# Hybrid attention / SSD / convolution block: the decays inside the SSD's chunks computed by scans on VectorE over rows spread by DMA, in place of split products with triangles on TensorE

## The chip, the cores and the metric

The kernel runs on one core of one Trainium2 chip. The time is the device time of one execution in microseconds (us); the page and the trace below come from one further execution that was profiled. TensorE (PE, with its weight loads as PEld), VectorE (DVE), ScalarE (ACT), GpSimd (POOL) and SyncE (SP, which here issues all the DMAs) run side by side, each through its own queue in its own fixed order.

## The reference

Two layers, each on 512 latent and 256 context tokens of 1024 channels. A layer projects the normalised input, feeds three branches (attention, a bidirectional SSD, a convolution module), gates and merges them, and projects back. The part that matters here is the SSD's work inside a chunk of 128 tokens, for 8 heads and two directions:

```
def segsum(x):
    t = x.shape[-1]
    xe = jnp.broadcast_to(x[..., :, None], x.shape + (t,))
    xs = jnp.cumsum(jnp.where(jnp.tril(jnp.ones((t, t), bool), -1), xe, 0.0), axis=-2)
    return jnp.where(jnp.tril(jnp.ones((t, t), bool)), xs, -jnp.inf)
...
    a = (dt * a_head).reshape(b, nc, SSD_CHUNK, h).transpose(0, 3, 1, 2)
...
    lmat = jnp.exp(segsum(a)).astype(x.dtype)
    cb = jnp.einsum('bclhn,bcshn->bhcls', cc, bc)
    y_diag = jnp.einsum('bhcls,bcshp->bclhp', cb * lmat, xd)
```

So for each chunk, head and direction a 128 x 128 matrix is needed whose entry (s, l) is the sum of `a` over the tokens after s up to l. Its exponential is the decay from token s to token l.

## The kernel before

All matrix products of the projections are made in three TensorE passes over split numbers: each weight tile is loaded as float32 (`raw`, three buffers), ScalarE rounds it (`whi`, L156), VectorE takes the rest (`wlo`, L157), and the matmuls run hh x whi, hh x wlo, hl x whi (`mm_cm_steps`, L175). The order on TensorE is written out by hand for most of a layer (`manual_schedule`). The other engines' orders and the DMA queue's are set by the scheduler of the framework from its own estimate of the times, with priorities; weight loads have a high one.

The SSD's inner loop stands in `Chunk` and in the list `main`. The first layer has 6 chunks (two of context, four latent), the second has 4. Each chunk has `begin` (L741, the products of C and B, masked into `gm`), two `decay(g)` (L751, one for each group of 4 heads), two `inner(g)` (L777, the matmuls `pyd` that use the weights `wt` of `decay`) and `end` (L790). That is 12 decays in the first layer and 8 in the second, 20 in all. `inner(g)` comes two steps behind its `decay(g)` (`ahead = 2`), and after every step `sf.fill` gives TensorE a piece of other work: the merge of the convolution branch (`merge_steps`, tiles `ps_gm` and `ps_br`) and the attention gates (`ps_ga`). So TensorE always has projections between the SSD's steps.

One `decay(g)` does this for each of the two directions: ScalarE makes four tiles `am` (a triangle of ones times the rounded `da` of a head, L759), VectorE makes `al` (the same triangle times the rest of `da`, L761), and TensorE multiplies `am` and `al` by a strict triangle (L764). All four products add up in one PSUM bank, `pseg`, which then holds for each head the forward sums above the diagonal and the backward sums below it. ScalarE takes the exponential (`ew`, L767), VectorE and ScalarE build `wt` from `gm` and the step sizes (L771, L772) and multiply by `ew` (L774):

```
for j, part in enumerate((am, al)):
    T.matmul(pseg[:, 0:512], m_gt if d == 0 else m_lt, part.rearrange("p h l -> p (h l)"),
             start=(d == 0 and j == 0), stop=(d == 1 and j == 1))
```

`small` (L83) gives tiles of 2 KB a partition from a ring of seven called W2. `am`, `al`, `ew`, `wt`, `xd` (the states' input, L722), the pieces of q and k on their way (`qs`, `qhl`, `khl`), `pth` of attention, the residual rows `xr` and others share it. `y0` (L781) is the one large GpSimd operation of a chunk.

Of the kernel before, what the change touches and what calls it, by code (L numbers as in the profile page):

```python
# [9 lines left out]
F32 = mybir.dt.float32  # L10
# [5 lines left out]
P = 128  # L16
# [41 lines left out]
def hybrid_kernel(ctx, tc, xT, cc, consts, rope, mod_params, params, fnw, w_mod, w_cm, w_q, w_kvd, w_z,  # L58
# [24 lines left out]
    def small(shape, dt, name):  # L83
        return wk.tile(shape, dt, tag="W2", name=name, bufs=7)
# [40 lines left out]
    mr = const.tile([P, 3 * P], F32R, name="mr")  # L125
    S.activation(mr, mraw, AF.Copy)
    m_gt, m_lt, identr = mr[:, 0:P], mr[:, P:2 * P], mr[:, 2 * P:3 * P]
# [185 lines left out]
    z_dr = [dr.tile([P, 512], F32, name=f"zdr{k}") for k in range(NTT)]  # L313
    y_dr = [dr.tile([P, NT], F32, name=f"ydr{k}") for k in range(KD)]

    mods = [sm.tile([P, 24, 2], F32, tag="mod", name=f"mod{i}", bufs=2) for i in range(2)]
    for li in range(2):
# [127 lines left out]
        na = sm.tile([P, 16], F32, tag="na", name="na")  # L445
        S.activation(na, par[:, O_AL:O_AL + 16], AF.Exp)
# [33 lines left out]
        dah = sm.tile([P, NTT, 16], F32R, tag="dah", name="dah")  # L480
        dal = sm.tile([P, NTT, 16], F32, tag="dal", name="dal")
        V.tensor_copy(dah, da)
        V.tensor_tensor(out=dal, in0=da, in1=f(dah), op=ALU.subtract)

# [67 lines left out]

        pc = pot("pc_cum")
# [3 lines left out]
        T.matmul(pcv[:, 1, :, 0:8], f(m_gt), da[:, :, 0:8], start=True, stop=True)  # L557
        T.matmul(pcv[:, 1, :, 8:16], f(m_lt), da[:, :, 8:16], start=True, stop=True)
# [176 lines left out]
        class Chunk:  # L735
# [15 lines left out]
            def decay(self, g):  # L751

                c, gm2 = self.c, self.gm2
                pseg = pwt("pseg")
                for d, m in enumerate((m_le, m_ge)):
                    h0 = d * 8 + g * 4
                    am = small([P, 4, P], F32R, "am")
                    for i in range(4):
                        S.activation(am[:, i, :], m, AF.Copy, scale=f(dah)[:, c, h0 + i:h0 + i + 1])  # L759
                    al = small([P, 4, P], F32R, "al")  # L760
                    V.tensor_tensor(out=al, in0=m.unsqueeze(1).to_broadcast([P, 4, P]),  # L761
                                    in1=dal[:, c, h0:h0 + 4].unsqueeze(2).to_broadcast([P, 4, P]), op=ALU.mult)
                    for j, part in enumerate((am, al)):
                        T.matmul(pseg[:, 0:512], m_gt if d == 0 else m_lt, part.rearrange("p h l -> p (h l)"),  # L764
                                 start=(d == 0 and j == 0), stop=(d == 1 and j == 1))
# [496 lines left out]
```

## Time and profile before

| | |
|---|---|
| median of 3 runs | 1495.2 us (1494.25 to 1498.19) |
| the profiled execution's own time | 1495.54 us |
| its span | 1493.8 us |
| busy: PE, PEld, DVE, ACT, POOL | 1450.1, 1255.5, 1039.1, 721.9, 81.6 us |
| PE busy by fortieths of the span | 5999999999999999999999989999999999999997 |
| moved by DMA | 172.58 MB, 116 GB/s over the span |

The span is what the profiler saw between the first and the last instruction; 1.7 us of the execution's time lie around it. Busy time counts an instruction from its start to its end. Matmuls overlap each other, so TensorE's pace is read from the distance between the starts of two matmuls, not from the length of one. An engine's idle time is listed with what ended it.

### The profile page before, as it was taken

How to read it: one execution, taken by the hardware profiler on the slowest of the kernel's cores; microseconds unless marked ns; L12 is line 12 of the kernel's file. 1: busy time of each engine (PE TensorE's matmuls, PEld its weight loads, DVE VectorE, ACT ScalarE, POOL GpSimd, SP SyncE). 2: the span in 40 equal slices, each digit the busy share in tenths (PEclk: the TensorE clock that was granted, in tenths of full speed). 3: DMA queues.
4: the chain of work that ended last, by engine and by line, in shares of the span. 5: the costliest groups of instructions: out<-in, count | busy, mean ns of one | idle time of the engine just before them, and what ended most of it. 6: DMA issues, size and time to landing. Idle time of an engine off the chain costs nothing.

```text
span 1493.8 us, 25061 instructions
## 1 busy us (share of the span) xinstructions
PE 1450.1 (97%) x9716; PEld 1255.5 (84%) x9716; DVE 1039.1 (70%) x1911; ACT 721.9 (48%) x1624; POOL 81.6 (5%) x177
## 2 busy tenths in 40 slices
PE   5999999999999999999999989999999999999997
PEld 4889899988888888888888877989988887888886
DVE  4689998666568675555344377899977788666564
ACT  4423543364445475555333154355455557666341
POOL 0000010100002110000000000001010021000000
PEclk9999999999999999999999999999999999999998
DMA  9222333223233322323652532213423242322542
GB/s 377 69 72 94 108 117 111 76 71 103 100 114 123 124 94 99 121 64 121 226 176 92 173 114 86 82 57 110 152 78 106 96 151 78 105 85 91 185 141 78
DMA packets 69687, 172.58 MB, mean 116 GB/s; under 512 B 7872, under 2 KB 24384, under 8 KB 69568
## 3 DMA queue, kind: packets, MB, share of 16 engines
q1 hardware_dynamic: 69568, 170.98, 34.8%
q8 instruction: 76, 1.25, 0.3%
q14 instruction: 43, 0.35, 0.1%
HBM read 143.43 MB, written 27.53 MB: 114 GB/s over the span
## 4 chain that ended last, share of the span: by engine, by line
PE 91%; DMA 2%; DVE 2%; ACT 2%; issue 1%; SPq 0%; POOL 0%; POOLq 0%; DVEq 0%; ACTq 0%
PE ps_gm L175 23%; PE ps_br L175 11%; PE ps_xbc L175 9%; PE ps_o L175 6%; PE ps_gcv L175 4%; PE ps_g L175 4%; PE ps_u L175 4%; PE po_v L1042 3%; PE ps_ga L175 3%; PE pt_p L1028 3%; PE ps_l L982 2%; PE ps_mod L229 2%; PE ps_z L216 1%; PE ps_q L216 1%; PE ps_q L217 1%; PE ps_z L217 1%
## 5 line engine op out<-in xcount | busy, mean ns | idle before, releaser
L156 ACT ACTIVATE whi<-raw 128x512 fp32r<-128x512 f32 (+1 forms) x316 | 199.0, 632 | 280.8 <-PE ps_gm L175 63.8
L157 DVE TENSOR_TENSOR wlo<-raw,whi 128x512 fp32r<-128x512 f32 (+1 forms) x316 | 216.9, 690 | 148.0 <-ACT whi L156 144.0
L175 PE MATMUL ps_gm<-hh,whi 128*128 128x512 f32 (+1 forms) x576 | 212.6, 369 | 0.0
L408 DVE SCALAR_TENSOR_TENSOR vacc<-vt,par,vacc 128x783 f32<-128x783 f32 (+1 forms) x232 | 206.5, 890 | 8.1 <-ACT vacc L405 4.5
L175 PE MATMUL ps_gm<-hh,wlo 128*128 128x512 f32 (+1 forms) x576 | 210.1, 365 | 0.0
L175 PE MATMUL ps_gm<-hl,whi 128*128 128x512 f32 (+1 forms) x576 | 209.6, 364 | 0.0
L175 PEld LDWEIGHTS ps_gm<-hh,whi 128*128 128x128 f32 x576 | 109.0, 189 | 16.4 <-issue 3.1
L175 PEld LDWEIGHTS ps_gm<-hh,wlo 128*128 128x128 f32 x576 | 109.0, 189 | 15.1 <-issue 1.7
L175 PEld LDWEIGHTS ps_gm<-hl,whi 128*128 128x128 f32 x576 | 109.0, 189 | 13.8 <-issue 0.9
L175 PE MATMUL ps_xbc<-hh,whi 128*128 128x512 f32 (+1 forms) x240 | 83.0, 346 | 0.0
L175 PE MATMUL ps_xbc<-hh,wlo 128*128 128x512 f32 (+1 forms) x240 | 82.1, 342 | 0.0
L175 PE MATMUL ps_xbc<-hl,whi 128*128 128x512 f32 (+1 forms) x240 | 82.0, 342 | 0.0
L1034 ACT ACTIVATE pth<-pt_p 128x512 f32<-128x512 f32 x72 | 43.6, 605 | 55.8 <-PE pt_p L1028 55.7
L653 ACT ACTIVATE tg<-ps_gm,hw 128x512 f32<-128x512 f32 x72 | 44.2, 614 | 51.1 <-PE ps_gm L175 51.1
L175 PE MATMUL ps_o<-yh,whi 128*128 128x256 f32 (+1 forms) x208 | 65.8, 317 | 1.5 <-DVE xnew L1105 1.4
L175 PE MATMUL ps_o<-yl,whi 128*128 128x256 f32 (+1 forms) x208 | 65.7, 316 | 0.0
L175 PE MATMUL ps_o<-yh,wlo 128*128 128x256 f32 (+1 forms) x208 | 65.7, 316 | 0.0
L522 DVE SCALAR_TENSOR_TENSOR xacc<-xraw,par,xacc 128x770 f32<-128x770 f32 (+1 forms) x64 | 63.4, 999 | 3.0 <-ACT xacc L519 2.8
L682 DVE SCALAR_TENSOR_TENSOR tg<-tg,ps_br 128x512 f32<-128x512 f32 x66 | 39.6, 600 | 34.0 <-PE ps_br L175 30.5
L1028 PE MATMUL pt_p<-mr,pe 128*128 128x128 f32 x416 | 62.4, 272 | 0.0
L988 DVE TENSOR_REDUCE mx<-ps_l 128x1 f32<-128x512 f32 x64 | 44.1, 690 | 24.1 <-PE ps_l L982 23.4
L1028 PEld LDWEIGHTS pt_p<-mr,pe 128*128 128x128 f32 x416 | 50.9, 140 | 11.7 <-issue 0.2
(276 smaller groups left out, 3661.7 us busy)
## 6 DMA issues: line engine op xcount, KB each, us to landing
raw<-in_w_cm_dram SPq DMA_DIRECT2D x96, 512.0 KB, 3.6
raw<-in_w_mod_dram SPq DMA_DIRECT2D x32, 512.0 KB, 3.6
raw<-in_w_br_dram SPq DMA_DIRECT2D x24, 512.0 KB, 3.7
raw<-in_w_out_dram SPq DMA_DIRECT2D x21, 512.0 KB, 3.7
wm<-in_w_mod_dram SPq DMA_DIRECT2D x16, 512.0 KB, 9.2
ydr<-tg SPq DMA_DIRECT2D x16, 384.0 KB, 4.9
yo<-ydr SPq DMA_DIRECT2D x16, 384.0 KB, 3.8
raw<-in_w_z_dram SPq DMA_DIRECT2D x8, 512.0 KB, 3.9
```

Source lines behind the costliest of these rows:

```text
L156: S.activation(hi, raw[:, u0:u0 + m, :], AF.Copy)
L157: V.tensor_tensor(out=lo, in0=raw[:, u0:u0 + m, :], in1=f(hi), op=ALU.subtract)
L175: T.matmul(ps[:, :b - a], st[:, col], mv(k)[:, a:b], start=(n == 0), stop=(n == len(order) - 1))
L216: T.matmul(ps[:, :ncol], xh(k)[:, t], hi, start=(k == 0), stop=False)
L408: V.scalar_tensor_tensor(out=acc[:, :n] if j else vt[:, o:o + n], in0=vt[:, o + j:o + j + n], scalar=cw(j), in1=acc[:, :n], op0=ALU.mult, ...
L522: xm = V.scalar_tensor_tensor(out=acc[:, :n], in0=raw[:, j:j + n], scalar=par[:, O_SCW + ct * 5 + j:O_SCW + ct * 5 + j + 1], in1=acc[:, :n ...
L653: lambda ps, a, b: S.activation(tg[:, a:b], ps, AF.Tanh, scale=0.5, bias=hw[:, br * 8 + ct:br * 8 + ct + 1]), "ps_gm")
L682: V.scalar_tensor_tensor(out=tg[:, a:b], in0=tg[:, a:b], scalar=1.0, in1=ps, op0=ALU.add, op1=ALU.mult)
L988: V.tensor_reduce(out=mx[:, 0, j:j + 1], in_=pl[j], axis=AX.X, op=ALU.max, negate=True)
L1028: T.transpose(pt[:, tok(2 * i + j)], pes[j][:, tok(k1 + i)], ident)
L1034: S.activation(pf, pt, AF.Copy)
L1042: T.matmul(po[64 * j:64 * j + 64, 0:P], vv[:, k0 + k1 + i, g, :], pth[:, i, j, :], start=(k1 + i == 0), stop=(k1 + i == nk - 1), tile_posi ...
```

## The change

In place of the split products, `da` is transposed once in each layer (`pt_a`, one transpose on TensorE), copied by ScalarE (`ar`) and written to DRAM as 96 rows of 128 (`a_dr`: a row for each chunk, direction and head). `decay(g)` then loads, for each direction, the four rows of its heads into all 128 partitions (`ab`, 128 x 512, by a DMA with top priority), and VectorE runs a scan along each partition: state = (state + a) x mask. The mask `m_wide` is a strict triangle, repeated four times, so partition s starts to sum behind token s and each head starts anew at zero; the backward direction scans the reversed row. GpSimd adds the two directions, and ScalarE takes the exponential from SBUF.

```
-    mr = const.tile([P, 3 * P], F32R, name="mr")
-    S.activation(mr, mraw, AF.Copy)
-    m_gt, m_lt, identr = mr[:, 0:P], mr[:, P:2 * P], mr[:, 2 * P:3 * P]
+    identr = const.tile([P, P], F32R, name="identr")
+    S.activation(identr, mraw[:, 2 * P:3 * P], AF.Copy)
+    m_wide = const.tile([P, 2, 4 * P], F32, name="m_wide")
+    for i in range(2):
+        V.tensor_copy(m_wide[:, i, :].rearrange("p (h l) -> p h l", h=4),
+                      mraw[:, i * P:(i + 1) * P].unsqueeze(1).to_broadcast([P, 4, P]))
+    m_gt, m_lt = m_wide[:, 0, 0:P], m_wide[:, 1, 0:P]
...
     def small(shape, dt, name):
-        return wk.tile(shape, dt, tag="W2", name=name, bufs=7)
+        return wk.tile(shape, dt, tag="W2", name=name, bufs=6)
...
-        dah = sm.tile([P, NTT, 16], F32R, tag="dah", name="dah")
-        dal = sm.tile([P, NTT, 16], F32, tag="dal", name="dal")
-        V.tensor_copy(dah, da)
-        V.tensor_tensor(out=dal, in0=da, in1=f(dah), op=ALU.subtract)
...
+        pa = pot("pt_a")
+        T.transpose(pa[0:NTT * 16, 0:P], da.rearrange("p t j -> p (t j)"), ident)
+        ar = small([P, P], F32, "ar")
+        S.activation(ar[0:NTT * 16, :], pa[0:NTT * 16, 0:P], AF.Copy)
+        nc.sync.dma_start(a_dr, ar[0:NTT * 16, :])
...
             def decay(self, g):
-                pseg = pwt("pseg")
-                for d, m in enumerate((m_le, m_ge)):
+                seg = []
+                for d in range(2):
                     h0 = d * 8 + g * 4
-                    am = small([P, 4, P], F32R, "am")
-                    for i in range(4):
-                        S.activation(am[:, i, :], m, AF.Copy, scale=f(dah)[:, c, h0 + i:h0 + i + 1])
-                    al = small([P, 4, P], F32R, "al")
-                    V.tensor_tensor(out=al, in0=m.unsqueeze(1).to_broadcast([P, 4, P]),
-                                    in1=dal[:, c, h0:h0 + 4].unsqueeze(2).to_broadcast([P, 4, P]), op=ALU.mult)
-                    for j, part in enumerate((am, al)):
-                        T.matmul(pseg[:, 0:512], m_gt if d == 0 else m_lt, part.rearrange("p h l -> p (h l)"),
-                                 start=(d == 0 and j == 0), stop=(d == 1 and j == 1))
+                    ab = small([P, 4 * P], F32, "ab")
+                    with tc.high_priority(offset=TOP):
+                        nc.sync.dma_start(ab, a_dr[c * 16 + h0:c * 16 + h0 + 4, :].rearrange("h l -> (h l)")
+                                          .unsqueeze(0).to_broadcast([P, 4 * P]))
+                    m = m_wide[:, 1 - d, :]
+                    av, mv = (ab, m) if d == 0 else (ab[:, ::-1], m[:, ::-1])
+                    V.tensor_tensor_scan(out=av, data0=av, data1=mv,
+                                         initial=0.0, op0=ALU.add, op1=ALU.mult)
+                    seg.append(ab)
+                G.tensor_tensor(out=seg[0], in0=seg[0], in1=seg[1], op=ALU.add)
                 ew = small([P, 4, P], F32, "ew")
-                S.activation(ew.rearrange("p h l -> p (h l)"), pseg, AF.Exp)
+                S.activation(ew.rearrange("p h l -> p (h l)"), seg[0], AF.Exp)
```

`na` (the negative exponentials of `A_log`) is now made in place in the parameter tile. The change moves instructions at three places.

TensorE, before, at the first decay of the first layer:

```order
L175 MATMUL ps_gm<-hh,whi 128x512
L175 MATMUL ps_gm<-hl,whi 128x512
L764 MATMUL pseg<-am,mr 128x512
L764 MATMUL pseg<-al,mr 128x512
L764 MATMUL pseg<-am,mr 128x512
L764 MATMUL pseg<-al,mr 128x512
L175 MATMUL ps_gm<-hh,wlo 128x512
```

TensorE, now, at the same place (L180 is the former L175):

```order
L180 MATMUL ps_gm<-hh,whi 128x512
L180 MATMUL ps_gm<-hl,whi 128x512
L180 MATMUL ps_gm<-hh,wlo 128x512
L180 MATMUL ps_gm<-hh,whi 128x512
L180 MATMUL ps_gm<-hl,whi 128x512
```

The four matmuls are gone, and what stood around them now stands together. This is so at all 20 decays; the rest of the order written by hand is as before.

VectorE, before, in the second layer, where the first decay ends (`wt`) and the second begins (`al`; `gm` are the masked products of C and B, `uc` a part of the convolution branch):

```order
L761 TENSOR_TENSOR al<-cst,dal 128x512 x2
L772 SCALAR_TENSOR_TENSOR wt<-gm_11583,dts,wt 128x128 x4
L748 TENSOR_TENSOR gm_11667<-pg,cst 128x256 x2
L603 TENSOR_TENSOR uc<-lv,uc 128x512
L774 TENSOR_TENSOR wt<-wt,ew 128x512
L157 TENSOR_TENSOR wlo<-raw,whi 128x512
```

VectorE, now, at the same place (the scans are listed as SCALAR_TENSOR_TENSOR of L772; L162, L611, L756, L782, L784 are the former L157, L603, L748, L772, L774):

```order
L782 SCALAR_TENSOR_TENSOR wt<-gm_11443,dts,wt 128x128 x4
L772 SCALAR_TENSOR_TENSOR ab<-ab,m_wide 128x512
L611 TENSOR_TENSOR uc<-lv,uc 128x512
L772 SCALAR_TENSOR_TENSOR ab<-ab,m_wide 128x512
L756 TENSOR_TENSOR gm_11515<-pg,cst 128x256
L162 TENSOR_TENSOR wlo<-raw,whi 128x512
L756 TENSOR_TENSOR gm_11515<-pg,cst 128x256
L784 TENSOR_TENSOR wt<-wt,ew 128x512
```

The two scans of the next decay stand ahead of the multiplication that ends the present one.

The DMA queue, now, in the second layer near its end of the SSD (`ydr` and `szc` wait for other engines, `raw` are weights):

```order
L153 DMA raw<-in_w_cm_dram 128x1024
L768 DMA ab<-adr 128x512 x2
L704 DMA ydr_161<-tg 128x512
L153 DMA raw<-in_w_cm_dram 128x1024 x2
L897 DMA ks<-kdr_131 128x128
```

The 40 loads of `ab` stand singly or in pairs between the weight loads, and each is issued only when those ahead of it in the queue have been.

## Rows read from the trace of the kernel before

**Rows 1.** The page: span, busy time of each engine, and TensorE's granted clock.

```profile
span 1493.8 us, 25061 instructions
...
PE 1450.1 (97%) x9716; PEld 1255.5 (84%) x9716; DVE 1039.1 (70%) x1911; ACT 721.9 (48%) x1624; POOL 81.6 (5%) x177
...
PEclk9999999999999999999999999999999999999998
```

**Rows 2.** Waits, weight loads, 262 to 520: waited for; total us, times, longest.

```profile
PEld pseg L764 <- ACT am L759: 0.9, 2, 0.6
...
PEld pseg L764 <- DVE al L761: 0.5, 1, 0.5
```

**Rows 3.** Waits, weight loads, 1083 to 1232: the only row.

```profile
PEld ps_br L175 <- DVE uc L603: 0.3, 1, 0.3
```

**Rows 4.** Stretches: length, PE, PEld, DVE, ACT, POOL busy (instructions), clock, DMA.

```profile
270.00:470.00 200.00, 199.07 (x1261) 172.92 (x1260) 131.32 (x260) 103.87 (x264) 18.80 (x31) 1.00 0.30 96
1083.00:1195.00 112.00, 112.00 (x535) 92.95 (x534) 84.64 (x156) 63.44 (x150) 11.81 (x22) 1.00 0.29 93
1232.00:1270.00 38.00, 35.44 (x229) 28.63 (x228) 31.25 (x74) 27.31 (x67) 5.51 (x6) 0.96 0.26 80
```

**Rows 5.** Waits of ScalarE, 1083 to 1232: its rounded weights wait for TensorE.

```profile
ACT whi L156 <- PE ps_gm L175: 28.4, 14, 4.3
```

**Rows 6.** Time order, PE, first decay: start us, us, instruction.

```profile
318.72 0.40 PE L764 MATMUL pseg<-am,mr 128*128 128x512 f32 x1
...
319.65 0.39 PE L175 MATMUL ps_gm<-hh,wlo 128*128 128x512 f32 x1
```

**Rows 7.** Groups of instructions: count | busy us, mean ns | idle before.

```profile
L759 ACT ACTIVATE am<-cst,dah 128x128 fp32r<-128x128 f32 x160 | 49.9, 390 | 5.2 <-DMA qdr<-qv 3.7 <-PE ps_st L726 0.9 <-DVE wt L774 0.5
L761 DVE TENSOR_TENSOR al<-cst,dal 128x512 fp32r<-128x512 f32 x40 | 27.1, 684 | 5.6 <-PE pseg L764 4.6 <-PE ps_st L726 0.9
```

**Rows 8.** Time order, 329 to 333 and 361: a GpSimd operation and VectorE.

```profile
330.71 1.04 POOL L781 TENSOR_TENSOR y<-xt,par 128x512 f32<-128x512 f32 x1 [12.52 <-DVE wt L772]
331.08 1.21 DVE L774 TENSOR_TENSOR wt<-wt,ew 128x512 f32<-128x512 f32 x1
...
361.43 0.69 DVE L774 TENSOR_TENSOR wt<-wt,ew 128x512 f32<-128x512 f32 x1
```

**Rows 9.** One line's instructions, L963 and L809: ns min/median/max, first and last start.

```profile
L963 PE MATMUL pt_us<-mr,xt x40: 270/272/331, 504.0 to 1233.5; 128*128 128x128 f32 x40
L809 DVE TENSOR_SCALAR xt<-y,ssr x10: 475/486/491, 359.1 to 1226.4; 128x512 f32<-128x512 f32 x10
```

**Rows 10.** DMA issues: count, KB each, median us to landing.

```profile
szc<-zdr SPq DMA_DIRECT2D x10, 256.0 KB, 3.8
```

**Rows 11.** Waits of the DMA queue, 262 to 500, then 1085 to 1240.

```profile
SPq L148 <- DVE wlo L157: 82.8, 11, 12.6
SPq L148 <- DVE wlo L157: 66.1, 16, 10.4
```

**Rows 12.** Time order, ScalarE: first and last of 12, then of 8, exponentials.

```profile
319.85 0.60 ACT L767 ACTIVATE ew<-pseg 128x512 f32<-128x512 f32 x1 [2.29 <-PE pseg L764]
466.44 0.58 ACT L767 ACTIVATE ew<-pseg 128x512 f32<-128x512 f32 x1
1114.71 0.60 ACT L767 ACTIVATE ew<-pseg 128x512 f32<-128x512 f32 x1
1195.17 0.60 ACT L767 ACTIVATE ew<-pseg 128x512 f32<-128x512 f32 x1
```

**Rows 13.** Time order: the first `wt` is done, and TensorE first uses it.

```profile
323.43 0.69 DVE L774 TENSOR_TENSOR wt<-wt,ew 128x512 f32<-128x512 f32 x1
336.13 1.00 PE L785 MATMUL pyd<-xt,wt 128*128 128x64 f32 x8
```

**Rows 14.** Waits of PE, 0 to 60.

```profile
PE ps_mod L229 <- DMA wm<-in_w_mod_dram: 13.5, 1, 13.5
```

More of the change, by code (lines that the diff above doesn't have):

```diff
@@ L313, in hybrid_kernel @@
     z_dr = [dr.tile([P, 512], F32, name=f"zdr{k}") for k in range(NTT)]
+    a_dr = dr.tile([NTT * 16, P], F32, name="adr")
     y_dr = [dr.tile([P, NT], F32, name=f"ydr{k}") for k in range(KD)]
@@ L443, in hybrid_kernel @@
         man.__enter__()
-        na = sm.tile([P, 16], F32, tag="na", name="na")
-        S.activation(na, par[:, O_AL:O_AL + 16], AF.Exp)
+        na = par[:, O_AL:O_AL + 16]
+        S.activation(na, na, AF.Exp)
         V.tensor_scalar(out=na, in0=na, scalar1=-1.0, scalar2=None, op0=ALU.mult)
@@ L556, in hybrid_kernel @@
         T.matmul(pcv[:, 0, :, 8:16], m_ge, da[:, :, 8:16], start=True, stop=True)
-        T.matmul(pcv[:, 1, :, 0:8], f(m_gt), da[:, :, 0:8], start=True, stop=True)
-        T.matmul(pcv[:, 1, :, 8:16], f(m_lt), da[:, :, 8:16], start=True, stop=True)
+        T.matmul(pcv[:, 1, :, 0:8], m_gt, da[:, :, 0:8], start=True, stop=True)
+        T.matmul(pcv[:, 1, :, 8:16], m_lt, da[:, :, 8:16], start=True, stop=True)
         T.matmul(pcv[:, 2], ones, da, start=True, stop=True)
```

## Prediction
> **What bounds the kernel now.** [...] Busy matmuls overlap, so 97% proves little; the list of waits has to say whether TensorE waits for anybody. In the first layer's SSD stretch its weight loads waited 0.9 us for `am` and 0.5 us for `al` [rows 2]; in the second layer's 0.3 us in all [rows 3]. The other way round, ScalarE's rounded weights waited 28.4 us for TensorE to free a buffer [rows 5]: the weights are made ahead and queue before TensorE. So TensorE is the bound in both stretches, at full clock, with VectorE at 131.3 of 200 us (66%) and 84.6 of 112 us (76%) [rows 4]. A matmul taken out there should come off the end, as long as VectorE and the loads keep up.
>
> **The change part by part.** The sum is made against the profiled execution, 1495.5 us, which is 0.3 us above the median of the three runs shown.
>
> *TensorE, removed.* A decay had four matmuls of `pseg`. The first starts at 318.72, the matmul after the fourth at 319.65 [rows 6]: 0.93 us for four, 0.232 us each. Their weight loads lie beside the matmuls. 20 decays make 80 matmuls and **18.6 us**. The waits for `am` and `al` (1.4 us) may go too; I leave them out of the sum and use them for the low end.
>
> *TensorE, added.* Two transposes of `da`, one a layer. The nearest row is a 128 x 128 transpose, 0.272 us long [rows 9]; between 0 and 0.3 us each. I take 0.1 each, as they overlap their neighbours: +0.2.
>
> *ScalarE, removed.* 160 `am`, 49.9 us [rows 7]. ScalarE was not the bound (63.4 of 112 us) [rows 4], so this is worth nothing by itself. The exponentials stay; the two copies of `ar` are small and made well ahead.
>
> *VectorE.* 40 `al` of 0.684 us go (27.1 us) [rows 7]; 40 scans come. No row shows a scan. Below, it costs what a two-input operation of its shape costs, 0.68 us. Above I set twice that, 1.37: each element needs the result of the one before it, which no operation of the kernel before does. I take the upper end, since that recurrence is just what sets it apart from its nearest row. Net, +0.69 us a scan: 24 x 0.69 = 16.6 us in the first layer, 16 x 0.69 = 11.0 in the second. [...]
>
> *GpSimd.* 20 additions of 128 x 512, by the nearest row 1.04 us each [rows 8], on an engine that is nearly idle. But the same rows show a price: `wt<-wt,ew`, which lasts 0.69 us alone, lasted 1.21 us when it started beside GpSimd's `y`, and ended 0.54 us after it. Between 0 and 1.04 us of VectorE are lost for each addition; I take the 0.52 us seen: 6.2 us in the first layer, 4.2 in the second.
> [...]
>
> *VectorE's account.* First layer: 131.3 + 16.6 + 6.2 = 154.1 us of work in 200 - 48 x 0.232 = 188.9 us, 82%. Second layer: 84.6 + 11.0 + 4.2 = 99.8 us in 112 - 32 x 0.232 = 104.6 us, 95%. The first is covered. The second is tight, and what hides it is the lead: the first `wt` was ready at 324.1 and used at 336.1 [rows 13], 12 us later. When the lead is used up, `pyd` on TensorE is late next, and the rounded weights after it. For short waits I put 2 us, between 0 and the first rival's price.
>
> *DMA queue.* 40 loads of 256 KB; the nearest row, `szc`, lands 3.8 us after issue [rows 10]. They stand among the weight loads, which wait for VectorE to free a `raw` buffer: 82.8 us over 11 waits and 66.1 over 16, 7.5 and 4.1 us each [rows 11]. An `ab` behind one of those comes that much later, and an `ab` that waits for a W2 slot holds up the weights behind it. The weights are ahead by what its waits show [rows 5], the decays by two steps; I cost this at nothing and give the case where the cover is gone as the second rival. The two writes of `adr` and W2's six buffers for seven are costed at nothing too: a decay now takes four tiles of W2 (two `ab`, `ew`, `wt`) where it took six.
>
> *Start.* Two copies onto `m_wide` stand ahead of the last two additions of the norm; a one-input operation of that size takes 0.49 us [rows 9], so 1.0 us on VectorE. TensorE waits 13.5 us for the first weights there anyway [rows 14], and later weights still arrive. Between 0 and 1.5 us; I take 0.5.
>
> **Sum:** 1495.5 - 18.6 + 0.2 + 0.5 + 2 = 1479.6; against the median 0.3 less, **1479**.
>
> **The rivals.**
> *VectorE becomes the bound in the second layer.* If every addition stops VectorE for its whole 1.04 us, its work there is 84.6 + 11.0 + 8.3 = 103.9 us; with 8 of its present 27 idle us left the stretch lasts its old 112 us, and the second layer's 7.4 us are lost: 1479 + 7, **1486**. For it: the 95% above. Against it: 0.52 us was seen, not 1.04, and VectorE may run ahead.
> *The loads set the pace (slower).* If a pair of `ab` can be loaded only after the decay before has freed its slots, one decay takes a wait behind weights, the landing, two scans, the addition, the exponential and the product: in the first layer 7.5 + 3.8 + 2.7 + 1.0 + 0.6 + 0.7 = 16.3 us, in the second 12.9. The decays are spaced (466.4 - 319.9)/11 = 13.3 us and (1195.2 - 1114.7)/7 = 11.5 us [rows 12], and 0.9 less with the matmuls gone: 12.4 and 10.6. The first layer would fall behind by 12 x 3.9 = 47 us less a lead of two steps, 25: 22 us of waiting on TensorE. The second would fall behind by 18 us, which its lead of 21 covers. 1479 + 22 = **1501**. It decides from 16 us a decay in the first layer. Against it: in the new order on VectorE the scans of the next decay stand ahead of the present product, so the next pair must be there already.
> *The gain is given back on the way to attention (no change).* At 1232 to 1270 TensorE already misses 2.6 us, and the clock falls to 0.96 [rows 4], since the queries' preparation on VectorE and ScalarE is as long as the filling work. If that preparation comes no earlier than now, because VectorE's queue is fuller and W2 has six slots, TensorE gains only the wait: up to 18 us back in the two layers, **1497**.
> That the matmuls aren't really gone is ruled out: the order shows none of the 80.
>
> **How the numbers follow.** Main case 0.70, VectorE the bound 0.13, loads set the pace 0.10, given back 0.07. A measurement of this kernel can tell some 0.3% (4.5 us) from no change. Faster by more: the main case and the first rival, 0.83; within it 0.07; slower 0.10. The range takes in the main case and the first rival, with their unknowns: low, no waits at all and those for `am` and `al` gone, 1495.2 - 18.6 - 1.4 - 0.5 of rounding, about 1474; high, the first rival with 6 us more for a scan or a load at its upper end, 1492.
>
> **What would show it.** Right: 80 fewer matmuls; weight loads in both stretches waiting under some 2 us for `wt`; the filling matmuls at 0.23 us; scans of 0.7 to 1.4 us; VectorE over 80% in the first stretch and over 90% in the second; some two-input operations drawn out to 1.2 us beside GpSimd. Wrong: waits of `pyd` for `wt` of more than 5 us in all (with VectorE full: the first rival; with VectorE idle until `ab` lands: the second), scans well over 1.4 us, or TensorE idle longer than 2.6 us before attention.

## The result and the profile after

The changed kernel takes 1529.4 us (median of 4 runs, 1526.9 to 1534.0) beside 1495.2 us for the kernel before in the same series: ratio 1.0221, 95% interval 1.0202 to 1.0240. By that ratio it is slower by 33 us (2.2%; the two medians lie 34.2 us apart), outside the predicted range, and on the side to which the prediction gave 0.10. The profiled execution is the slowest of the four, 1534.0 us.

The page of the kernel after, its first rows, beside [rows 1]:

```profile
span 1532.2 us, 24897 instructions
...
PE 1457.8 (95%) x9638; PEld 1260.9 (82%) x9638; DVE 1066.1 (70%) x1909; ACT 679.1 (44%) x1468; POOL 111.4 (7%) x197
...
PEclk9999999998999999999999989999999998999999
```

The matmuls of `pseg` are gone: 9638 for 9716, 80 fewer and the two transposes more. Yet TensorE is busy 7.7 us longer, so the other matmuls took longer. VectorE is at 70% as before, so over the whole span it is not the bound.

Stretches of the two kernels, from the first `pg` to about the first `pt_us` of each layer. The columns are those of [rows 4]. Before:

```profile
315.00:504.00 189.00, 188.07 (x1188) 162.98 (x1187) 133.31 (x278) 96.39 (x256) 23.80 (x30) 1.00 0.34 111
1110.00:1228.00 118.00, 118.00 (x561) 98.16 (x560) 95.03 (x198) 66.18 (x169) 15.45 (x20) 1.00 0.34 110
```

After:

```profile
320.60:525.60 205.00, 189.63 (x1141) 162.93 (x1140) 145.72 (x273) 69.81 (x164) 38.36 (x39) 0.93 0.41 128
1136.00:1262.00 126.00, 115.25 (x525) 94.98 (x524) 104.32 (x198) 49.12 (x112) 25.46 (x27) 0.96 0.41 127
```

The first stretch is 16 us longer where 11 us should have gone. TensorE stands still for 15.4 of its 205 us (0.9 before), and its mean clock fell from 1.00 to 0.93 of full speed. Who it waits for there (waits of PE after, 320 to 526, then 1136 to 1262; total us, times, longest):

```profile
PE ps_br L180 <- ACT tg L661: 6.3, 3, 3.4
PE ps_st L734 <- DVE xd L731: 3.4, 1, 3.4
PE ps_gm L180 <- DVE tg L690: 3.0, 3, 2.3
...
PE ps_gm L180 <- ACT tg L661: 5.9, 2, 3.3
PE ps_gm L180 <- DVE wlo L162: 3.1, 1, 3.1
```

None of it is `pyd` waiting for `wt`, the sign I had named. `tg` is the tanh (ScalarE) and the product (VectorE) of the *filling* matmuls: the operations that empty a PSUM bank (evacuate it) so that the next filling product can start. They make 15.2 of the 26.1 us that TensorE stood still in the two stretches; `xd`, which VectorE makes for the states, makes 5.2. Before, the longest wait of TensorE in the first of these stretches was 0.4 us. The new operations, by groups after (count | busy us, mean ns | idle before):

```profile
L772 DVE TENSOR_TENSOR_SCAN ab<-ab,m_wide 128x512 f32<-128x512 f32 x40 | 48.7, 1220 | 32.4 <-DMA ab<-adr 32.3
...
L777 ACT ACTIVATE ew<-ab 128x512 f32<-128x512 f32 x20 | 12.6, 631 | 75.9 <-POOL ab L775 75.9
```

VectorE stood still 32.3 us for the loads of `ab`, ScalarE 75.9 us for GpSimd's additions. Both engines have enough idle time for that: by the page they are busy 1066.1 and 679.1 of 1532.2 us. What stands behind the waiting instruction in their fixed order has none to spare. Here is one such wait, 365 to 374 us after, in order of time (PE, ACT, DVE and POOL taken apart):

```profile
365.53 0.28 PE L180 MATMUL ps_gm<-hh,wlo 128*128 128x256 f32 x1
...
369.29 0.40 PE L180 MATMUL ps_br<-uc,wlo 128*128 128x512 f32 x1
373.05 0.79 PE L180 MATMUL ps_br<-uc,whi 128*128 128x256 f32 x2 [3.36 <-ACT tg L661]
...
365.60 0.62 ACT L161 ACTIVATE whi<-raw 128x512 fp32r<-128x512 f32 x1
370.88 0.63 ACT L817 ACTIVATE y<-y 128x512 f32<-128x512 f32 x1 [4.66 <-DVE y L815]
...
372.00 0.63 ACT L777 ACTIVATE ew<-ab 128x512 f32<-128x512 f32 x1 [0.40 <-POOL ab L775]
372.54 0.46 ACT L661 ACTIVATE tg<-ps_gm,hw 128x256 f32<-128x256 f32 x1
...
367.11 1.22 DVE L772 TENSOR_TENSOR_SCAN ab<-ab,m_wide 128x512 f32<-128x512 f32 x1 [0.24 <-DMA ab<-adr]
...
369.04 1.23 DVE L772 TENSOR_TENSOR_SCAN ab<-ab,m_wide 128x512 f32<-128x512 f32 x1
370.18 0.67 DVE L815 TENSOR_TENSOR y<-y,szc 128x512 f32<-128x512 f32 x1
370.76 1.75 DVE L162 TENSOR_TENSOR wlo<-raw,whi 128x512 fp32r<-128x512 f32 x1
...
370.49 1.48 POOL L775 TENSOR_TENSOR ab<-ab 128x512 f32<-128x512 f32 x1 [5.75 <-DVE ab L772]
```

The last `ps_gm` matmul ended at 365.8, and ScalarE was free at 366.2. Yet it made the tanh only at 372.54: ahead of it stood a square that waited for VectorE (whose product came behind two scans), and `ew`, which waited for GpSimd. TensorE, done with the rest at 369.7, stood for 3.36 us until the tanh had freed its bank. The order had been fixed by the scheduler from its own estimate of the times. No row shows that estimate; I take it that scans and loads came later than it said, and that what TensorE needed therefore stood behind them.

This wait costs more than itself. Windows of 4 us around it, columns as in [rows 4]:

```profile
365.00:369.00 4.00, 4.00 (x25) 3.47 (x25) 3.68 (x7) 1.22 (x3) 0.00 (x0) 1.00 0.35 113
369.00:373.00 4.00, 0.69 (x3) 0.20 (x2) 3.81 (x4) 1.72 (x5) 2.34 (x3) 0.88 0.00 0
373.00:377.00 4.00, 3.95 (x24) 3.71 (x28) 2.79 (x9) 1.79 (x5) 0.19 (x1) 0.50 0.65 197
377.00:381.00 4.00, 3.53 (x22) 2.52 (x15) 3.46 (x7) 0.28 (x1) 0.00 (x0) 0.50 0.46 159
381.00:385.00 4.00, 4.00 (x17) 3.27 (x16) 0.16 (x1) 0.00 (x0) 0.00 (x0) 0.84 0.18 71
```

After 3.36 us of standing, the granted clock is 0.50 for 8 us: a loss of about 4 us more, an estimate from these rows. Other waits cost less. After one of 2.65 us the clock was 0.50 for 6 us, after one of 2.61 us it stayed at 1.00 (first and second row; the waits end at 427.23 and 1195.88 us):

```profile
427.00:433.00 6.00, 5.77 (x18) 4.91 (x19) 3.04 (x4) 1.58 (x4) 0.00 (x0) 0.50 0.64 156
1196.00:1205.00 9.00, 9.00 (x43) 7.47 (x44) 7.40 (x15) 1.36 (x3) 1.63 (x3) 1.00 0.26 95
```

### The profile page after: what moved, and what is told of

Its sections match the earlier page's. It is cut to its first block, busy times and chain, and to the rows that moved or that the text cites. A ratio compares the mean times of both kernels' runs of the same rounds, so it can differ in the third digit from the quotient of the medians.

```text
span 1532.2 us, 24897 instructions
## 1 busy us (share of the span) xinstructions
PE 1457.8 (95%) x9638; PEld 1260.9 (82%) x9638; DVE 1066.1 (70%) x1909; ACT 679.1 (44%) x1468; POOL 111.4 (7%) x197
## 5 line engine op out<-in xcount | busy, mean ns | idle before, releaser
L162 DVE TENSOR_TENSOR wlo<-raw,whi 128x512 fp32r<-128x512 f32 (+1 forms) x316 | 222.5, 709 | 132.2 <-ACT whi L161 130.2
L180 PE MATMUL ps_gm<-hh,whi 128*128 128x512 f32 (+1 forms) x576 | 216.2, 375 | 8.9 <-ACT tg L661 5.9
L180 PE MATMUL ps_gm<-hh,wlo 128*128 128x512 f32 (+1 forms) x576 | 213.6, 371 | 3.1 <-DVE wlo L162 3.1
L180 PE MATMUL ps_gm<-hl,whi 128*128 128x512 f32 (+1 forms) x576 | 212.6, 369 | 0.0
L180 PEld LDWEIGHTS ps_gm<-hh,whi 128*128 128x128 f32 x576 | 111.4, 193 | 26.6 <-ACT tg L661 6.2
L180 PEld LDWEIGHTS ps_gm<-hh,wlo 128*128 128x128 f32 x576 | 110.8, 192 | 19.3 <-DVE wlo L162 3.7
L180 PEld LDWEIGHTS ps_gm<-hl,whi 128*128 128x128 f32 x576 | 111.1, 193 | 14.3 <-issue 0.9
L180 PE MATMUL ps_xbc<-hh,whi 128*128 128x512 f32 (+1 forms) x240 | 83.0, 346 | 0.0
L180 PE MATMUL ps_xbc<-hh,wlo 128*128 128x512 f32 (+1 forms) x240 | 82.1, 342 | 0.0
L180 PE MATMUL ps_xbc<-hl,whi 128*128 128x512 f32 (+1 forms) x240 | 82.0, 342 | 0.0
L772 DVE TENSOR_TENSOR_SCAN ab<-ab,m_wide 128x512 f32<-128x512 f32 x40 | 48.7, 1220 | 32.4 <-DMA ab<-adr 32.3
L180 PE MATMUL ps_o<-yh,whi 128*128 128x256 f32 (+1 forms) x208 | 65.9, 318 | 2.2 <-DVE xnew L1115 1.5
L180 PE MATMUL ps_o<-yh,wlo 128*128 128x256 f32 (+1 forms) x208 | 65.6, 316 | 0.0
L180 PE MATMUL ps_o<-yl,whi 128*128 128x256 f32 (+1 forms) x208 | 65.6, 316 | 0.0
L661 ACT ACTIVATE tg<-ps_gm,hw 128x512 f32<-128x512 f32 x72 | 44.1, 612 | 41.9 <-PE ps_gm L180 41.9
L180 PE MATMUL ps_br<-uc,whi 128*128 128x512 f32 (+1 forms) x192 | 56.5, 379 | 6.4 <-ACT tg L661 6.3
L1038 PE MATMUL pt_p<-identr,pe 128*128 128x128 f32 x416 | 62.3, 272 | 0.0
L690 DVE SCALAR_TENSOR_TENSOR tg<-tg,ps_br 128x512 f32<-128x512 f32 x66 | 39.5, 599 | 32.7 <-PE ps_br L180 28.1
```

What stands on the lines that cost most here:

```text
L162: V.tensor_tensor(out=lo, in0=raw[:, u0:u0 + m, :], in1=f(hi), op=ALU.subtract)
L180: T.matmul(ps[:, :b - a], st[:, col], mv(k)[:, a:b], start=(n == 0), stop=(n == len(order) - 1))
L661: lambda ps, a, b: S.activation(tg[:, a:b], ps, AF.Tanh, scale=0.5, bias=hw[:, br * 8 + ct:br * 8 + ct + 1]), "ps_gm")
L690: V.scalar_tensor_tensor(out=tg[:, a:b], in0=tg[:, a:b], scalar=1.0, in1=ps, op0=ALU.add, op1=ALU.mult)
L772: V.tensor_tensor_scan(out=av, data0=av, data1=mv, initial=0.0, op0=ALU.add, op1=ALU.mult)
L1038: T.transpose(pt[:, tok(2 * i + j)], pes[j][:, tok(k1 + i)], ident)
```

## The experiments

Theories. **Queue order:** the chain load, scan, addition, exponential runs through four queues of fixed order, and TensorE waits for evacuations that stand behind a link. **Buffers:** W2 has six for seven. **VectorE's work or contention:** scans and additions are too much, or GpSimd's additions stop VectorE. **Small gain:** the 18.6 us were never there. All runs were timed against the kernel before on the same chip; "against before" is the ratio less one, times 1497 us (1495 for the changed kernel). Differences between runs are taken from that column; those of the medians differ from them by up to some 2 us.

| run | median us | ratio, 95% interval | against before, us |
|---|---|---|---|
| changed kernel | 1529.4 | 1.0221 (1.0202 to 1.0240) | +33.0 |
| e1 before, W2 of six | 1509.1 | 1.0073 (1.0049 to 1.0096) | +10.9 |
| e2 before, no decays | 1485.4 | 0.9923 (0.9900 to 0.9946) | -11.5 |
| e3 no addition | 1512.0 | 1.0101 (1.0077 to 1.0125) | +15.1 |
| e4 no loads | 1499.8 | 1.0021 (1.0004 to 1.0038) | +3.1 |
| e5 addition on VectorE | 1524.0 | 1.0170 (1.0148 to 1.0192) | +25.4 |
| e6 no loads, no addition | 1495.1 | 0.9988 (0.9977 to 0.9998) | -1.8 |
| e7 W2 of seven | 1514.7 | 1.0116 (1.0099 to 1.0134) | +17.4 |
| e8 exponential in place | 1534.3 | 1.0244 (1.0226 to 1.0261) | +36.5 |
| e9 loads that nobody reads | 1527.8 | 1.0210 (1.0189 to 1.0231) | +31.4 |
| e10 own ring for ab | 1536.1 | 1.0252 (1.0226 to 1.0279) | +37.7 |
| e11 ab in W | 1522.3 | 1.0169 (1.0150 to 1.0187) | +25.3 |
| e12 seven, addition on VectorE | 1506.1 | 1.0071 (1.0045 to 1.0098) | +10.6 |
| e13 exponential behind tanh | 1508.3 | 1.0079 (1.0054 to 1.0104) | +11.8 |
| e14 e12 and e13 together | 1496.1 | 0.9997 (0.9981 to 1.0012) | -0.4 |
| e15 e14 with ab in W | 1503.3 | 1.0039 (1.0026 to 1.0053) | +5.8 |
| e16 e14, last decays as they were | 1493.9 | 0.9981 (0.9968 to 0.9995) | -2.8 |
| e17 e16, addition on GpSimd | 1507.0 | 1.0078 (1.0057 to 1.0099) | +11.7 |

Where the time goes, from one profiled execution each: how much longer than in the kernel before TensorE takes from one mark to the next. The marks are the start, the first `pg`, the first `pt_us`, the last `pc_cum`, the last `pt_us` and the last `ps_o`. The profiled executions of the changed kernel and of e16 are some 4 us longer than the medians of these kernels (1534.0 and 1497.7 us), so single columns are good to a few microseconds only.

| run | to pg | first SSD | to pc_cum of layer two | second SSD | rest |
|---|---|---|---|---|---|
| changed kernel | +5.6 | +16.0 | +4.3 | +8.4 | +4.7 |
| e1 | +2.3 | +4.8 | +4.5 | +0.1 | +2.8 |
| e2 | 0.0 | -9.0 | +2.6 | -5.2 | +0.1 |
| e4 | +1.6 | -1.9 | -0.6 | -1.0 | +4.7 |
| e9 | +19.8 | +1.0 | -1.0 | +11.4 | +2.2 |
| e11 | -0.7 | +7.8 | +5.6 | +8.9 | +6.3 |
| e13 | +5.8 | -1.2 | +1.3 | +5.2 | +3.6 |
| e14 | +0.5 | -4.9 | +1.0 | +3.7 | +1.3 |
| e16 | -0.2 | -6.8 | -0.4 | +2.7 | +7.0 |
| e17 | +3.3 | +0.5 | +0.9 | +0.8 | +7.5 |

### What the two halves are worth: e1, e2

e1, in the kernel before:

```
-        return wk.tile(shape, dt, tag="W2", name=name, bufs=7)
+        return wk.tile(shape, dt, tag="W2", name=name, bufs=6)
```

> The kernel before with one edit: W2 has six buffers in place of seven. If the loss comes from the chain load, scan, addition, exponential, which stands in four queues in a fixed order (the chain theory), the ring is a side matter here: 1495 us, within 5 of the kernel before. If the smaller ring is what hurts (the ring theory), the part of the loss that lies outside the SSD's stretches, 4.5 us at the layers' border and 4.6 us in attention, and some of that inside shows here too: 1505 us or more.

+10.9 us. I had costed this edit at nothing. By the table of marks it is lost in several places, the second SSD not among them. What delays TensorE at each was not followed.

e2, in the kernel before (the loop with `am`, `al` and `pseg` taken out):

```
-                pseg = pwt("pseg")
...
-                S.activation(ew.rearrange("p h l -> p (h l)"), pseg, AF.Exp)
+                S.activation(ew, m_ge.unsqueeze(1).to_broadcast([P, 4, P]), AF.Exp)
```

> The kernel before without am, al and pseg; the exponential is taken of a resident triangle, so the decays are left out. It prices the prediction's one gain by itself, with nothing put in its place. If TensorE is the bound as I said, 18.6 us of matmuls and 1.4 us of waits go: 1476 us, between 1472 and 1480. If something else had taken the gain anyway (rival): 1488 us or more, and then the change lost only half of what it seems to have lost.

The gain is 11.5 us (8 to 15), not 18.6, and the time lies between the two ranges that were expected. The first SSD gives 9.0 of 11.1 us and the second 5.2 of 7.4, and 2.6 come back in between. New waits of PE, 300 to 1300, in the place of nothing or 0.6 us:

```profile
PE ps_br L175 <- ACT tg L653: 2.8, 2, 2.1
...
PE pt_qk L845 <- ACT kk L846: 1.8, 1, 1.8
PE ps_br L175 <- DVE uc L603: 1.8, 1, 1.8
```

TensorE moves up to operations of other engines that come no earlier. The third rival (given back before attention) had the kind right. It named the queries, and `kk`, of the keys, belongs there, but most of these waits lie elsewhere.

### Links taken out: e3, e4, e6

e3 drops `G.tensor_tensor(out=seg[0], ...)`. e4:

```
-                        nc.sync.dma_start(ab, a_dr[c * 16 + h0:c * 16 + h0 + 4, :]...)
-                    V.tensor_tensor_scan(out=av, data0=av, data1=mv, ...)
+                    V.tensor_tensor_scan(out=av, data0=mv, data1=mv, ...)
...
+                S.activation(..., seg[0], AF.Exp, scale=-1.0)
```

e6 is both.

> The changed kernel without GpSimd's addition: the exponential takes the forward scan alone, so the backward sums are left out of it; loads and scans all stay. Chain theory: ScalarE's 75.9 us of waiting for the addition shrink to waits for the scan, and what TensorE lost to tanh evacuations that stand behind the exponential goes: 1505 to 1515 us. Contention theory (what hurts is that each addition stops VectorE): 20 x 1.04 us at most come back: 1510 to 1520. If the loads alone make the loss: 1525 to 1530, no change.

> The changed kernel without the 40 loads of ab: both scans read the resident mask in place of the spread rows, so the right rows are left out; scans, additions and exponentials stay, with the same shapes. Chain theory: the 32.3 us that VectorE waited for loads go and with them what stood behind the scans (layer norm, tanh products): 1490 to 1505 us. VectorE-work theory (40 scans and 20 additions are simply too much work): 1520 to 1530, as the work is unchanged.

> The changed kernel without the loads of ab and without the addition: both scans read the resident mask, the exponential takes one of them, so the right rows and the backward sums are left out. Without loads alone 29.6 us came back, without the addition alone 17.4. If these are two separate links whose costs add up: 1529.4 - 29.6 - 17.4 = 1482 us, near the 1485 of the kernel before without its decays. If they hide each other (the same waits of TensorE, ended last now by one, now by the other), or if the ring of six sets a floor: 1493 to 1500.

Without the loads 29.9 us come back, without the addition 17.9, without both 34.8. So the two are links of one chain and not separate costs: once no scan waits for rows, the addition costs 4.9 us. e4 rules out that the scans' work alone makes the loss: all 40 are there, and the kernel is 3 us off the one before. But without its load `ab` holds its buffer only from the scan on, so the 29.9 us are the price of the wait for rows and of the buffers that loads hold, together. e6 against e2 differs by 9.7 us, about what the six buffers cost in e1 (10.9). If the two can be compared, that leaves nothing for the scans; as costs do not add up here, this is argued. e3 by its time alone can't tell the chain from contention.

### Buffers: e7, e8, e10, e11

e7 (`m_wide` in bfloat16 and two small matmuls replaced make the room):

```
-        return wk.tile(shape, dt, tag="W2", name=name, bufs=6)
+        return wk.tile(shape, dt, tag="W2", name=name, bufs=7)
```

e8 writes the exponential onto the sum (`S.activation(seg[0], seg[0], AF.Exp)`). e10 and e11:

```
-                    ab = small([P, 4 * P], F32, "ab")
+                    ab = wk.tile([P, 4 * P], F32, tag="AB", name="ab", bufs=2)    # e10
+                    ab = work([P, 4 * P], F32, "ab")                              # e11
```

> The changed kernel with seven buffers in W2 again. Room comes from the mask in bfloat16 (0 and 1 are exact in it) and from making the sums behind a token as total less running sum, on VectorE, in place of two small matmuls with the triangles. Ring theory: the 11.7 us that a ring of six cost the kernel before come back, and more, as each ab holds a buffer from its load on: 1510 to 1518 us. Chain theory: the waits are for data, not for buffers: 1523 to 1532.

> The changed kernel with the exponential written over the sum (ab) in place of a tile of its own: a decay takes three tiles of W2 in place of four, the ring stays at six. Ring theory: 1512 to 1520 us. Chain theory: 1523 to 1532. As this edit adds nothing elsewhere, it also shows whether the side edits of the run with seven buffers matter.

> As the run with loads that nobody reads, but the scans work in place on the loaded rows: ab has a ring of two buffers of its own, W2 keeps its six for the others. (The mask is again a view of hl, so the right masks are left out.) If the loads come late because ab stands in W2 behind xd, ew and wt (buffer theory): 1503 to 1512 us, most of the wait for data gone. If they come late whatever the ring, by landing time and by a pair of buffers that is free only after the exponential: 1520 to 1535.

> The changed kernel in full with one edit: ab is taken from the ring of six 3 KB buffers (W) that holds gm2, y0, y1 and szc, in place of W2. Buffer theory: W2 has two tenants fewer a decay and the loads find a buffer sooner, 1510 to 1520 us. If W is as full as W2 the wait only moves: 1525 to 1540.

The seventh buffer gives back 15.6 us. No run has e7's side edits alone; e1, which has none, lost 10.9 us by the same buffer, and the scans take as long with the mask in bfloat16 (1.218 us for 1.220). The other three missed the buffer theory's numbers, and e8 its rival's too. e8 is 3.5 us worse than the changed kernel: each loaded buffer now stays taken until the product `wt`, so fewer tiles did not mean earlier loads (argued, not shown). In e10, where `m_wide` is left out to make room and a view of `hl` serves as the mask, the loads stood in SyncE's queue for GpSimd's additions (25.5 us over 9 waits, 262 to 560) and for `ew`, with weights behind them. e11 tells most. What ScalarE (first row, us and times) and VectorE (second) waited for in it, by the view of the tile `ab`:

```profile
  POOL ab L775: 48.2, 18
  DMA ab<-adr: 6.6, 6
```

6.6 us for rows in place of 32.3, and yet only 7.7 us came back. So late rows by themselves are not the cause. ScalarE still waited 48.2 us for additions, but that is not what held up TensorE in this run. Waits of PE, 240 to 1300; then the longest in order of time:

```profile
PE ps_st L734 <- DVE xd L731: 15.9, 3, 9.3
PE ps_gm L180 <- DVE tg L690: 5.6, 2, 5.2
...
PE ps_br L180 <- ACT tg L661: 1.9, 1, 1.9
```

```profile
1143.72 2.04 PE L734 MATMUL ps_st<-xd,bt 128*128 128x256 f32 x4 [9.32 <-DVE xd L731]
...
1135.42 2.33 DVE L772 TENSOR_TENSOR_SCAN ab<-ab,m_wide 128x512 f32<-128x512 f32 x2
1137.67 1.68 DVE L784 TENSOR_TENSOR wt<-wt,ew 128x512 f32<-128x512 f32 x1
1139.27 2.06 DVE L772 TENSOR_TENSOR_SCAN ab<-ab,m_wide 128x512 f32<-128x512 f32 x1
...
1141.83 2.95 DVE L731 TENSOR_TENSOR xd<-xt,dd 128x512 f32<-128x512 f32 x3
```

VectorE was busy without a break from 1132 to 1144 us, with scans that had their rows ahead of the `xd` that TensorE needed, and some of its operations were drawn out (2.06 us for a scan that takes 1.22, 1.68 for a product that takes 0.69) while GpSimd was busy 5.0 of the 8 us from 1136. So in e11 a link of the chain delayed what stood behind it on VectorE too (the 9.32 us), and did so without waiting itself.

### Loads that nobody waits for: e9

```
+                    dead = wk.tile([P, 4 * P], F32, tag="AB", name="dead", bufs=2)
                     with tc.high_priority(offset=TOP):
-                        nc.sync.dma_start(ab, a_dr...)
+                        nc.sync.dma_start(dead, a_dr...)
```

> The loads of ab are made in full, at their places in the DMA queue, but into a ring of two buffers of their own that nobody reads; the scans, additions and exponentials run on resident data (a view of hl in place of the rows and of the mask, so right rows and masks are left out; sums behind a token as total less running sum). It splits the 29.6 us of the loads. If what hurts is VectorE standing still for their data: 1495 to 1503 us, as without loads. If their traffic or their places in the one DMA queue hurt (weights behind them come late): 1515 to 1530.

It does not split the 30 us as meant, though its time lies in the range for traffic and places in the queue. With no slot to wait for, the scheduler put all loads with top priority ahead of the SSD, where they delayed something else. SyncE's queue, then VectorE, at 275 to 291 us:

```profile
278.84 3.71 SPq L765 DMA_DIRECT2D dead<-adr  x3
282.60 0.43 SPq L591 DMA_DIRECT2D qdr<-qv  x1
...
286.10 0.69 DVE L727 TENSOR_TENSOR xd<-xt,dd 128x512 f32<-128x512 f32 x1 [4.81 <-DMA qdr<-qv]
290.19 1.23 DVE L769 TENSOR_TENSOR_SCAN ab<-hl 128x512 f32<-128x512 f32 x1 [3.41 <-DMA qdr<-qv]
```

The writes of `qdr` free W2 buffers; they stood behind the loads, `xd` behind them, the layer norm behind `xd`, and TensorE stood 17.0 us for `xn` in one piece. The first SSD itself then took 1.0 us more than before, with its loads already done. The second took 11.4 us more; 8.9 of them are one wait of TensorE for `ga`, a gate of attention made on VectorE, which was not followed further. Whether the loads' traffic costs anything while the SSD runs stays open: no run had the traffic there without scans that wait for it (e11, with 6.6 us of such waits, comes nearest).

### The addition on VectorE: e5, e12

```
-                G.tensor_tensor(out=seg[0], in0=seg[0], in1=seg[1], op=ALU.add)
+                V.tensor_tensor(out=seg[0], in0=seg[0], in1=seg[1], op=ALU.add)
```

> The changed kernel with the addition on VectorE in place of GpSimd: one queue fewer in the chain, and no operation of GpSimd beside the scans and products; VectorE gets 20 x 0.69 us more work. Chain theory: the addition follows the second scan at once, ScalarE's wait for it shrinks, 1512 to 1522 us. Rival, that VectorE has too much work: 1530 to 1540, as 14 us are added. Rival, that the addition beside VectorE is all of what leaving it out gave back (17 us): 1512 to 1516, as none of it then lies beside another.

> The run with seven buffers with the addition on VectorE besides. Seven buffers gave back 14.7 us, the addition on VectorE 5.4. If these are separate: 1529.4 - 14.7 - 5.4 = 1509 us. If seven buffers took away the waits in which GpSimd's addition mattered, VectorE's 14 us of added work show instead: 1515 to 1522.

7.6 us back in the changed kernel, 6.8 with seven buffers, though VectorE's 20 additions of 0.69 us are more work for it. The 1524.0 us of e5 lie between what the chain theory said (up to 1522) and what too much work on VectorE would have given (from 1530). Seven buffers and this move add up.

### The order on ScalarE: e13, e14, e15

```
+                with tc.issue_after(evac[0].ins):
+                    S.activation(ew.rearrange("p h l -> p (h l)"), self.seg[g], AF.Exp)
...
-                main.append(decays[j])
+                main.append(partial(both, weights[j - 1], decays[j]) if j else decays[j])
```

`evac[0]` is the tanh emitted last; `weights` are the second halves of the decays, from `ew` on.

> The changed kernel in full with one edit: each exponential (and the weights after it) is issued one step later than its scans, and on ScalarE behind the tanh of the filling product that was emitted last, so that no tanh that TensorE needs stands behind an exponential that waits for a scan or an addition. Queue theory (TensorE waits because the evacuations stand behind chain work in ScalarE's fixed order): the waits for tg of L661, some 12 us over both stretches with the slow clock after each, mostly go: 1512 to 1520 us. If these waits are only where a general lateness shows (the rows come late and VectorE is full), something else is late instead: 1525 to 1540.

> The run with seven buffers and the addition on VectorE (1506), with the exponentials behind the tanh besides. Queue theory: its four waits of about 3.3 us for tg of L661 go (13 us of idle TensorE with what the clock loses after them), 1490 to 1497 us, level with the kernel before. Rival, lateness: 1503 to 1512.

> As the run before it, with ab in the ring of 3 KB buffers (W), where VectorE waited only 6.6 us for rows. Queue theory: the scans no longer hold up VectorE's own evacuations and the exponentials no longer ScalarE's, 1485 to 1495 us, the floor being the kernel before without its decays (1485). Rival: W has no room to spare in attention's part, and what the SSD gains is lost there: 1500 to 1512.

e13 leaves loads, scans, additions and six buffers in place and moves each exponential, with the weights made from it, a step back and behind a tanh: 21.2 of the 33.0 us come back (1508.3 us, below the 1512 to 1520 expected), and the first SSD goes from +16.0 to -1.2 us. The five waits for ScalarE's `tg` in the two stretches (12.2 us) are gone from the list of waits; the first rows of PE, 300 to 1300, are now

```profile
PE ps_st L737 <- DVE xd L734: 5.5, 1, 5.5
PE pyd L803 <- DVE wt L792: 3.9, 2, 2.9
```

What VectorE (first row, us and times) and ScalarE (second) wait for in e13, by the view of the tile `ab`:

```profile
  DMA ab<-adr: 17.2, 11
...
  POOL ab L778: 8.9, 4
```

So it is the order that costs the time: with the exponentials behind the tanh, ScalarE waits 8.9 us for additions in place of 75.9, and the tanh comes when TensorE needs it. With seven buffers and the addition on VectorE the same move gives back 11.0 us (e14 against e12), and e14 is level with the kernel before. Two things are not parted by these runs. The edit moves the products `wt` on VectorE as well, and VectorE's wait for rows falls with it, from 32.3 to 17.2 us; that this fall is not what helped is argued from e11, where it fell to 6.6 and gave back 7.7 us. e15 fell to its rival.

### The rest: e16, e17

e14's end of the second SSD shows a late exponential:

```profile
1208.47 1.94 PE L803 MATMUL pyd<-xt,wt 128*128 128x64 f32 x8 [3.99 <-DVE wt L792]
...
1210.74 0.63 PE L179 MATMUL ps_gm<-hl,whi 128*128 128x512 f32 x1
1211.17 0.63 PE L179 MATMUL ps_gm<-hh,wlo 128*128 128x512 f32 x1
```

A wait of 4.0 us, and after it matmuls 0.43 us apart in place of 0.23. e16 emits `weights` of a layer's last two decays in their own step and not behind a tanh (shown against e14); e17 puts the addition back on GpSimd besides.

```
+        own = len(decays) - 2
...
-                main.append(partial(both, weights[j - 1], decays[j]) if j else decays[j])
+                main.append(partial(both, *weights[j - 1:min(j, own)], decays[j], *weights[max(j, own):j + 1]) if j else decays[j])
```

> The run with seven buffers, the addition on VectorE and the exponentials behind the tanh (1496), except that the last two decays of each layer keep their exponential in their own step, not behind a tanh. In that run the last exponential of the second layer came late, so that the last matmuls of pyd waited 4.0 us and the step from the last pg to pt_us took 8.2 us more than before. Queue theory: these 8 us go, 1487 to 1491 us, faster than the kernel before. Rival, that the lateness only moves on to the preparation of the queries: 1494 to 1498.

> As the run before it, with the addition back on GpSimd: VectorE is rid of 14 us of work, and the addition stands beside its operations again. Queue theory: with nothing that TensorE needs standing behind it, the place of the addition hardly matters, within 4 us of the run before it (1485 to 1494). Contention theory (20 additions hold up VectorE by up to 1.3 us each): 6 to 15 us slower than it.

e16 is the best version with scans: 0.9981 of the kernel before, an interval that just excludes no change, and less than the 0.3% I called distinguishable. Its time misses the 1487 to 1491 us of its theory and lies at the low end of the rival's. The wait for `pyd` is gone; others, of 9.0 us in two for `xd` and 4.0 us for `qhl`, take its place. `qhl` is the preparation of the queries that the rival named: from 1227.3 to 1265.3 TensorE misses 5.8 us at a clock of 0.82, where before, at the same place from the last `pt_us`, it missed 2.6 at 0.96 [rows 4]. e17 is 14.5 us slower than e16 (13.1 by the medians), in the range that contention was to give and far from the 4 us of the queue theory. The rows of the two pages, e16 and then e17:

```profile
PE 1439.7 (96%) x9630; PEld 1247.5 (83%) x9630; DVE 1065.0 (71%) x1935; ACT 675.9 (45%) x1466; POOL 85.5 (6%) x177
```

```profile
PE 1442.0 (96%) x9630; PEld 1248.7 (83%) x9630; DVE 1065.1 (71%) x1915; ACT 675.6 (45%) x1466; POOL 118.1 (8%) x197
```

In e17 VectorE has 20 additions fewer (14.4 us in e16) and is busy just as long: its other operations were drawn out by 14.5 us, 0.72 us for each addition on GpSimd. Not all of it need come from the additions: 4.7 us lie in ten `xt<-y,ssr` (0.49 us each in e16, 0.96 in e17), which took 0.79 us each in e3 too, without any addition. The same sum from the changed kernel (1066.1) and e3 (1056.8) gives 0.47 us, from e4 (1064.4) and e6 (1058.6) 0.29. That the drawn-out operations are what costs the 14.5 us is not shown: in e17 the chain also has one queue more, and ScalarE's `ew` waited 24.4 us for GpSimd's sum, where in e16 it waited 17.9 for VectorE's.

## Why the prediction was wrong

- **"80 matmuls and 18.6 us".** Right in kind, too big: e2 prices it at 11.5 us (8 to 15). Of what TensorE gains, it spends a part waiting for other engines that come no earlier (the rows at e2).
- **"The DMA queue ... I cost this at nothing".** This is the step that failed. With the buffers that they hold, the loads are worth 29.9 us here (e4), 16.9 without the addition (e3 less e6). I asked whether weights or `wt` would come late because of them, and had a rival for that. I did not ask what stands behind a scan that waits for a load on VectorE, and behind an exponential that waits on ScalarE. Before, `ew` waited for TensorE alone (18.7 us over 13 waits). Nor need a scan wait to do this: in e11 they had their rows, and TensorE stood 9.3 us for an `xd` behind them.
- **"For short waits I put 2 us".** The same omission on the other side: only `pyd` and the rounded weights were named as late next. Late next were the evacuations of the filling products, `tg` of L661 and L690, and `xd`. Moving the exponentials behind the tanh gives back 21.2 us (e13). The clock stood in no term: after six of the eight waits of 1.8 us or more in the two stretches it was at 0.50 to 0.63 for the next 2 to 8 us, and after the other two (1.80 and 2.61 us) at 1.00.
- **"W2's six buffers for seven ... costed at nothing".** 10.9 us in the kernel before (e1), 15.6 in the changed one (e7). Counting the tiles that a decay takes (four for six) was no argument: the ring also serves other stages (e1 loses time in four of the five columns), and `ab` holds a buffer from its load on.
- **Scans.** 1.22 us (mean of 40), inside 0.68 to 1.37; I took the upper end.
- **GpSimd's additions.** 0.52 us of VectorE each; measured 0.29, 0.47 and 0.72. The size was right, but its worth was put too low: I let VectorE carry it, and the addition's place on GpSimd costs the kernel 6.8 to 14.5 us (e5, e12, e17 less e16), by drawn-out operations or by the longer chain. That an addition stops VectorE for its whole length, as the first rival put it, was not shown. At 1.29 us, the additions' median, it would be 25.8 us over 20, an estimate; the three comparisons show 5.8 to 14.5.
- **VectorE's account.** 82% and 95% of the stretches; measured 145.72 of 205.0 us (71%) and 104.32 of 126.0 (83%), in stretches that are cut a little otherwise and had grown longer. Its total rose by 27.0 us, where 27.6 for the scans and 10.4 for the additions had been put. The first rival (VectorE the bound of the second layer) did not happen.
- **The start.** 0.5 us; the first `pc_cum` comes at 237.2 against 237.4 us: nothing.
- **The rival "the loads set the pace", 1501.** It had the side and the loads right, not the way: its delay was to reach TensorE through `pyd`, which waited for no `wt` in the changed kernel.
- **The rival "given back on the way to attention".** Its sign is there, as a small part: from 1266.3 to 1304.3 us TensorE misses 3.9 us at a clock of 0.87, where before it missed 2.6 at 0.96 [rows 4].

The parts do not add up to 33: seven buffers (15.6), ScalarE's order (21.2) and the addition's place (7.6) sum to 44.4, and together give 33.4 (e14). I take it that they end the same waits.

## What to carry to other kernels

Moving a reduction off TensorE is not just a count of busy time: here the new chain through other engines' queues delayed what stood behind its links (15.2 us of waits for evacuations, 5.2 for `xd`). So list, for each instruction of the chain, what TensorE needs that follows it in that engine's order: PSUM evacuations, and operands such as `xd`. If an engine has idle time but is ordered by estimated times, put the evacuations ahead of the chain explicitly (worth 21.2 us in e13). And before taking a buffer from a shared ring, look at every stage that uses the ring; the number of tiles is no price. (That the time for which a tile holds its buffer is the right price was not tested.)

## What was not expected of the hardware

- One short wait of TensorE cost about twice itself, by estimate: after its 3.36 us the granted clock was 0.50 for 8 us. After one of 2.65 us it was 0.50 for 6 us, after one of 2.61 us 1.00 for 9. The mean clock of the changed kernel is 0.977, of the one before 0.994.
- Moving GpSimd's 20 additions onto VectorE added nothing to VectorE's busy time: 1065.0 us with them, 1065.1 without (e16, e17).
